# Sums of the seven half-size products' left operands: by VectorE, or by accumulating transfers

## The chip, the cores and the metric

One core of a Trainium2 chip runs the whole program. The metric is the device time of one execution in microseconds, from launch to end; less is better. The profile speaks of TensorE (PE, with PEld for its weight loads), VectorE (DVE), ScalarE (ACT), GpSimd (POOL) and SyncE (SP). SP does nothing here but issue transfers; POOL issues some too.

## The reference

One step of a decoder layer: a mixer (gated-delta heads and mLSTM heads), an output projection, and a feed-forward block with a short causal convolution. Only the last one matters here:

```python
h = _rmsnorm(x, norm_ffn_g)
u = jnp.einsum('bld,df->blf', h, w_up)          # 2048 -> 2 * 5632
uc, ffn_new = _causal_dwconv(u, ffn_buf, ffn_conv_w)
uc = uc + ffn_conv_b
gate, up = jnp.split(uc, 2, axis=-1)
x = x + jnp.einsum('blf,fd->bld', silu(gate) * up, w_down)   # 5632 -> 2048
```

There are 512 prompt tokens and 8 x 8 sample tokens, 576 columns in all, and everything is float32.

## The kernel before

Activations lie transposed: features on the 128 partitions, the 576 tokens (NT) as columns in two halves of 288 (HALF). A float32 product is made of three float32r products: each operand is split into a high part (a cast on ACT, line 120) and the rest (a subtraction on DVE, line 121), and high x high, high x low and low x high are summed in PSUM. A matmul takes a 128 x 128 weight block and 288 columns.

The feed-forward block has these stages. The first three pairs of up-projection tiles (gate tile j and up tile NF + j, NF = 44) are made directly (`dense`, the third pair by `dense_pair`, line 198). The other 41 pairs use Winograd's form of Strassen's scheme: the 2 x 2 blocks are the two output tiles by the two halves of the inner dimension (left operand A11, A12, A21, A22, each a 128 x 1024 array of w_up, 512 KB in DRAM) and the two inner halves by the two token halves (right operand). Seven products of half size take the place of eight. The down projection is cut into the BLOCKS of line 29: blocks of 4 tiles are made directly (`down`, line 198), two blocks of 12 by the same seven products (`down_seven`), in 8 groups each, with left blocks of 128 x 768 (384 KB).

The right operands (seven sums of activations, split, in the tiles bh and bl of pools b1 and b2) are made once per stage, by `prep` (up) and `down_prep` (down), mostly on DVE. The left operands are made group by group by the generator `left_operands`: each `yield` ends one step, which makes one of the group's seven operands: `op(src)` casts and splits it into wh and wl. Every third operand has wh and wl in the stage's own pool (`ur` or `sx`), the others in the two buffers each of pool `wp`. The operands that are sums are made by `comb` on DVE (line 1248): in order A11, S1 = A21 + A22, S2 = S1 - A11, A12, S3 = A11 - A21, S4 = A12 - S2, A22. The four blocks are loaded on SP's queue into tiles `raw`, two in `wp`, the rest in the stage's pool.

`product` (line 1287) multiplies the oldest waiting operand with right sum b (24 matmuls up, 18 down) and then runs the next step, so that operands are three ahead of the products. A buffer of wh and wl comes free when the product three back is done. `pair` runs the seven products of a pair in the order b = 0, 4, 5, 2, 1, 3, 6, adds their results up on DVE as they come (p1, u2, u3, u4 hold partial sums), puts them into the padded rows of `conv_pads` (filled by POOL), and runs the convolution (`conv_rest`) and `hidden`, whose result is stored to DRAM on SP's queue by `later`. `down_seven` does the same and adds into the residual tiles x2.

The stage is entered by `seven_start`: it closes the pool of the dense activations (`ap`), opens `b2` and `ur` in the memory that comes free, and runs the first three steps between parts of `prep`. The first three products of the first pair (operands 0, 1 and 2) are begun together, k blocks 0 to 4 of each and then 5 to 7 (KB1 = 5), because the right operands of the last k blocks are made last. In the down projection `down` runs the first three steps during its last three output pairs (mp >= 5).

PE's order is the program's (a manual schedule). On the other engines and queues a scheduler orders the instructions by priority and by when they could start; work under `urgent` or `ahead` has a higher priority.

Of the kernel before, what the change touches and what calls it, by code (L numbers as in the profile page):

```python
# [13 lines left out]
P = 128  # L14
# [54 lines left out]
class Layer:  # L69
# [1048 lines left out]
    def ffn(self):  # L1118
        nc, I, O = self.nc, self.I, self.O
        V, A, Pl = nc.vector, nc.scalar, nc.gpsimd  # L1120
        fin = I["ffn_conv"].rearrange("p (s j) b w -> p s j (b w)", s=2)
        fout = O["ffn_conv"].rearrange("p (s j) b w -> p s j (b w)", s=2)
        rv = None
        self.bh, self.bl = [], []
        for j in range(NPL):
            hs = []
            for s in range(2):
                if j < NPL - 1:
                    pd = self.dense()
# [24 lines left out]
        for j in range(NPL, NF):  # L1154
            if j == NF - 1:
                first = [self.load_hidden(self.ur.tile([P, NT], F32, tag="raw", name=self.nm("h"), bufs=4), i) for i in range(FB)]
# [60 lines left out]

    def operands(self):

        def raw(j, t, u):  # L1220
            pool, n = (self.wp, 2) if self.nraw % 6 < 2 else (self.ur, 4)
            self.nraw += 1
            r = pool.tile([P, 1024], F32, tag="raw", name=self.nm("raw"), bufs=n)
            self.nc.sync.dma_start(out=r, in_=self.I["w_up"][2 * j + t][u])
            return r

        return self.left_operands(self.ur, 1024, [lambda t, u, j=j: raw(j, t, u) for j in range(NPL, NF)])

    def left_operands(self, pool, width, raws):
        V = self.nc.vector  # L1230
        nop = 0

        def op(src):
            nonlocal nop
            with self.urgent():
                hl = []
                for n in "hl":
                    if nop % 3 == 2:
                        hl.append(pool.tile([P, width], F32R, tag="w" + n, name=self.nm("w" + n)))
                    else:  # L1240
                        hl.append(self.wp.tile([P, 1024], F32R, tag="w" + n, name=self.nm("w" + n), bufs=2)[:, 0:width])
                nop += 1
                self.split(*hl, src)
            self.ops.append(hl)

        def comb(out, a, b, o):
            with self.urgent():
                V.tensor_tensor(out=out, in0=a, in1=b, op=o)  # L1248

        nxt = [raws[0](*tu) for tu in ((0, 0), (1, 0))]  # L1250
        for i, raw in enumerate(raws):
            a11, a21 = nxt
            a22, a12 = raw(1, 1), raw(0, 1)
            op(a11)
            yield
            s = pool.tile([P, width], F32, tag="s", name=self.nm("s"))
            comb(s, a21, a22, ALU.add)
            op(s)
            yield
            comb(s, s, a11, ALU.subtract)  # L1260
# [12 lines left out]
            op(a22)  # L1273
            yield

    def part(self, out, b, op, k0, k1, nk):
# [15 lines left out]
    def pair(self, j, fst, steps):  # L1292

        V, A = self.nc.vector, self.nc.scalar
        add = lambda o, a, b: V.tensor_tensor(out=o, in0=a, in1=b, op=ALU.add)
        e = lambda tag: self.up.tile([P, HALF], F32, tag=tag, name=self.nm(tag))
        rg, og = self.conv_pads(fst[:, 0, j - NPL])
        ru, ou = self.conv_pads(fst[:, 1, j - NPL])

        def product(b):  # L1300
            if j == NPL and b in (0, 4, 5):
                return begun.pop(0)
            out = bank(b)
            self.product(out, b, steps)
# [3 lines left out]
            return self.psd()[:, 0, 0:HALF] if b in (4, 3) else self.psr()[:, 0:HALF]  # L1308

        if j == NPL:  # L1310
            begun = [bank(b) for b in (0, 4, 5)]
            for k0, k1 in ((0, KB1), (KB1, 8)):
                for out, b, op in zip(begun, (0, 4, 5), self.ops):
# [5 lines left out]
        def evac(outs, x, y):  # L1319
            with self.urgent():  # L1320
                for o, p, r in zip(outs, self.psum_parts(x, x), self.psum_parts(y, y)):
                    if o is not None:
                        add(o, p, r)
# [24 lines left out]
    def load_hidden(self, t, j):  # L1348
# [92 lines left out]
    def down_operands(self, ns):  # L1441
# [14 lines left out]
        return self.left_operands(self.sx, n, [lambda t, u, mp=mp: raw(mp, t, u) for mp in range(8)])  # L1456

    def down_seven(self, steps, ns, f1):
        V, A = self.nc.vector, self.nc.scalar
        add = lambda o, a, b: V.tensor_tensor(out=o, in0=a, in1=b, op=ALU.add)  # L1460
        e = lambda tag: self.sx.tile([P, HALF], F32, tag=tag, name=self.nm(tag))
        for mp in range(8):
            if mp == 5:
# [5 lines left out]
                self.product(out, b, steps, KS)  # L1469
                return out  # L1470

            def acc(o, *vs):
                for v in vs:
                    add(o, v, o)

            with self.urgent():
                p1, u2, u3, u4 = (e(t) for t in ("p1", "u2", "u3", "u4"))
                ps = product(0)
                A.copy(p1, ps)
                p5 = product(4)  # L1480
                ps = product(5)
                add(u2, ps, p1)
                add(u4, p5, u2)
                ps = product(2)
                acc(x[0][0], ps, p1)
                ps = product(1)
                add(u3, ps, u2)
                acc(x[1][1], ps, u4)
                ps = product(3)
                acc(x[0][1], ps, u4)  # L1490
                ps = product(6)
                acc(x[1][0], ps, u3)
        return hs

    def down_last(self, acts):
# [164 lines left out]
```

## Time and profile before

| | |
|---|---|
| time, median of 3 runs | 2697.01 us (2695.82 to 2698.49) |
| the profiled execution's own time | 2699.44 us |
| its span, first to last instruction | 2697.7 us |
| up projection by seven products | 1229.9 to about 2154 us of the span |
| down blocks by seven products | 2206.9 to 2342 and 2395.6 to 2528.7 us |
| plain loads of w_up | 176 of 512 KB |

Windows rows read: the stretch and its length, then busy time and instructions (x) of PE, PEld, DVE, ACT and POOL, then the granted clock, the share of the DMA engines and GB/s. A timeline row reads: start, duration, engine, line, operation, output <- inputs, shape, count, and in brackets how long the engine had been idle before it and what ended that. Matmuls overlap, so the distance between two starts is what one costs, not the duration shown. A row of a wait list reads: who <- for whom: us in total, times, longest.

### The profile page before, as it was taken

To read this page: it belongs to the slowest core of one execution; us is meant where nothing else is said; L and a number is where in the kernel's file an instruction comes from. 1 tells how busy PE (TensorE), PEld (TensorE's weight loads), DVE (VectorE), ACT (ScalarE), POOL (GpSimd) and SP (SyncE) were. 2 spreads that over 40 slices of the span, in tenths; PEclk is the share of its full clock that TensorE was granted. 3 is DMA by queue.
4 is the path that set the end of the run, shared out by engine and by line. 5 is a ranking of instruction groups with operands and counts; after the bars stand their busy time and mean duration, and the time that the engine had idled before them with its cause. 6 is when DMAs were issued, how large, how long until landed. Compare 5 with 4: busy or idle time off the path is not lost.

```text
span 2697.7 us, 48872 instructions
## 1 busy us (share of the span) xinstructions
PE 2651.0 (98%) x19967; PEld 2607.0 (97%) x19967; DVE 1994.0 (74%) x3338; ACT 1080.2 (40%) x1704; POOL 333.6 (12%) x658
## 2 busy tenths in 40 slices
PE   7999999999999999998999999999999999999998
PEld 7998999999999999998999999999999999999998
DVE  7887777765544332389888888888888888888646
ACT  5334344443333322254444444444444433433324
POOL 3222322222211001101000000000000100000001
PEclk9999999999999999999999999999999999999999
DMA  5222222222333344444333333333333373342333
GB/s 195 85 77 87 90 91 91 91 88 92 114 113 104 115 135 135 135 123 150 107 111 108 108 108 108 108 108 108 108 108 109 109 256 94 106 146 71 122 97 100
DMA packets 112233, 304.02 MB, mean 113 GB/s; under 512 B 21912, under 2 KB 28184, under 8 KB 112008
## 3 DMA queue, kind: packets, MB, share of 16 engines
q1 hardware_dynamic: 107896, 291.17, 34.0%
q0 software_dynamic: 1872, 7.37, 0.8%
q8 instruction: 156, 2.56, 0.4%
q10 hardware_dynamic: 2240, 2.36, 0.3%
q14 instruction: 69, 0.57, 0.1%
HBM read 264.79 MB, written 36.06 MB: 112 GB/s over the span
## 4 chain that ended last, share of the span: by engine, by line
PE 89%; DVE 4%; DMA 1%; issue 0%; ACT 0%; POOL 0%; DVEq 0%; POOLq 0%; SPq 0%; ACTq 0%
PE pd L198 36%; PE pr L1283 31%; PE pd L1283 12%; PE pr L198 3%; PE pr L1509 1%; DVE bl L121 1%; DVE wl L121 1%; DMA r<-hid 0%; DVE r L1544 0%; PE pr L256 0%; PE pr L843 0%; PE pr L980 0%; PE pr L982 0%; PE pr L690 0%; PE pr L687 0%
## 5 line engine op out<-in xcount | busy, mean ns | idle before, releaser
L120 ACT CAST wh<-raw 128x1024 fp32r<-128x1024 f32 (+1 forms) x394 | 404.6, 1027 | 741.1 <-PE pd L198 400.2
L1283 PE MATMUL pr<-bh,wh 128*128 128x288 f32 x2120 | 626.8, 296 | 1.9 <-ACT bh L120 1.9
L1283 PE MATMUL pr<-bh,wl 128*128 128x288 f32 x2120 | 624.6, 295 | 0.5 <-DVE wl L121 0.5
L1283 PE MATMUL pr<-bl,wh 128*128 128x288 f32 x2120 | 624.3, 294 | 0.6 <-DVE bl L121 0.6
L121 DVE TENSOR_TENSOR wl<-raw,wh 128x1024 fp32r<-128x1024 f32 (+1 forms) x394 | 476.5, 1210 | 178.8 <-ACT wh L120 172.4
L198 PE MATMUL pd<-ah,wh 128*128 128x288 f32 x2496 | 560.3, 306 | 0.0
L198 PE MATMUL pd<-ah,wl 128*128 128x288 f32 x2496 | 534.5, 296 | 0.2 <-DVE wl L121 0.2
L198 PE MATMUL pd<-al,wh 128*128 128x288 f32 x2496 | 533.8, 296 | 0.0
L198 PEld LDWEIGHTS pd<-ah,wh 128*128 128x128 f32 x2496 | 401.0, 189 | 14.2 <-issue 7.7
L198 PEld LDWEIGHTS pd<-ah,wl 128*128 128x128 f32 x2496 | 401.8, 189 | 0.5 <-DVE wl L121 0.5
L198 PEld LDWEIGHTS pd<-al,wh 128*128 128x128 f32 x2496 | 401.7, 189 | 0.0
L1283 PEld LDWEIGHTS pr<-bl,wh 128*128 128x128 f32 x2120 | 400.0, 189 | 1.1 <-DVE bl L121 1.1
L1283 PEld LDWEIGHTS pr<-bh,wh 128*128 128x128 f32 x2120 | 398.4, 188 | 2.1 <-ACT bh L120 2.1
L1283 PEld LDWEIGHTS pr<-bh,wl 128*128 128x128 f32 x2120 | 398.9, 188 | 1.2 <-DVE wl L121 1.2
L120 ACT CAST wh<-s 128x1024 fp32r<-128x1024 f32 (+1 forms) x171 | 169.6, 992 | 361.2 <-DVE s L1248 142.2
L1283 PE MATMUL pd<-bh,wh 128*128 128x288 f32 x848 | 252.2, 297 | 5.6 <-ACT wh L120 5.6
L1283 PE MATMUL pd<-bh,wl 128*128 128x288 f32 x848 | 250.8, 296 | 1.7 <-DVE wl L121 1.7
L1283 PE MATMUL pd<-bl,wh 128*128 128x288 f32 x848 | 249.7, 294 | 0.0
L121 DVE TENSOR_TENSOR wl<-s,wh 128x1024 fp32r<-128x1024 f32 (+1 forms) x171 | 196.5, 1149 | 26.0 <-ACT wh L120 18.4
L1283 PEld LDWEIGHTS pd<-bh,wh 128*128 128x128 f32 x848 | 160.3, 189 | 6.1 <-ACT wh L120 6.1
L1283 PEld LDWEIGHTS pd<-bh,wl 128*128 128x128 f32 x848 | 160.6, 189 | 2.2 <-DVE wl L121 2.2
L1283 PEld LDWEIGHTS pd<-bl,wh 128*128 128x128 f32 x848 | 161.0, 190 | 0.0
(400 smaller groups left out, 3501.1 us busy)
## 6 DMA issues: line engine op xcount, KB each, us to landing
raw<-in_w_up SPq DMA_DIRECT2D x176, 512.0 KB
raw<-in_w_in SPq DMA_DIRECT2D x114, 512.0 KB
raw<-in_w_down SPq DMA_DIRECT2D x40, 512.0 KB
raw<-in_w_out SPq DMA_DIRECT2D x32, 512.0 KB
raw<-in_w_down SPq DMA_DIRECT2D x40, 384.0 KB
hid<-r SPq DMA_DIRECT2D x44, 288.0 KB
r<-hid SPq DMA_DIRECT2D x40, 288.0 KB
r<-in_xT SPq DMA_DIRECT2D x32, 288.0 KB
```

What stands on the lines that cost most here:

```text
L120: nc.scalar.copy(hi, src)
L121: nc.vector.tensor_tensor(out=lo, in0=src, in1=hi.bitcast(F32), op=ALU.subtract)
L198: mm(outs[hf], w, x[:, hf * HALF:(hf + 1) * HALF], start=first and i == 0, stop=last and i == 2)
L1283: mm(out, w[:, ks], x[:, sl], start=k == 0 and i == 0, stop=k == nk - 1 and i == 2)
L1509: mm(pr[:, 0:n], w[:, ks], acts[kk][:, a * NT + sl.start:a * NT + sl.stop], start=kk == 0 and i == 0, stop=kk == FB - 1 and i == 2)
```

## The change

The four sums of a group are no longer made by DVE. A block is loaded into a tile, and another block is added to it by a second transfer that accumulates into the tile (`nc.gpsimd.dma_start(..., accum_op=ALU.add)`, on POOL's queue). Since such a transfer only adds, the operands are those of the same scheme with the first block row's sign turned: A11, S1 = A21 + A22, A12, S1 + A11, A11 + A21, A22, S1 + A11 + A12. The sums of the products subtract where they added, and the products run in the order b = 0, 4, 2, 5, 1, 6, 3. Tile `s` has two buffers, `raw` in `ur` three instead of four, and in `sx` one instead of two. A group has four plain loads, as before, and four accumulating ones besides, so that each group reads its blocks from DRAM twice.

```diff
     def operands(self):
 
-        def raw(j, t, u):
-            pool, n = (self.wp, 2) if self.nraw % 6 < 2 else (self.ur, 4)
+        def raw(i, t, u):
+            pool, n = (self.wp, 2) if self.nraw % 5 < 2 else (self.ur, 3)
             self.nraw += 1
-            r = pool.tile([P, 1024], F32, tag="raw", name=self.nm("raw"), bufs=n)
-            self.nc.sync.dma_start(out=r, in_=self.I["w_up"][2 * j + t][u])
-            return r
+            return pool.tile([P, 1024], F32, tag="raw", name=self.nm("raw"), bufs=n)
...
-        nxt = [raws[0](*tu) for tu in ((0, 0), (1, 0))]
-        for i, raw in enumerate(raws):
-            a11, a21 = nxt
-            a22, a12 = raw(1, 1), raw(0, 1)
+        def load(i, t, u, r=None):
+            r = raw(i, t, u) if r is None else r
+            nc.sync.dma_start(out=r, in_=src(i, t, u))
+            return r
+
+        def add(r, i, t, u):
+            nc.gpsimd.dma_start(out=r, in_=src(i, t, u), accum_op=ALU.add)
+
+        def sums(i):
+            return load(i, 1, 0, pool.tile([P, width], F32, tag="s", name=self.nm("s"), bufs=2))
+
+        s, a11 = sums(0), load(0, 0, 0)
+        add(s, 0, 1, 1)
+        for i in range(n):
+            a12 = load(i, 0, 1)
             op(a11)
             yield
-            s = pool.tile([P, width], F32, tag="s", name=self.nm("s"))
-            comb(s, a21, a22, ALU.add)
+            add(a11, i, 1, 0)
             op(s)
             yield
-            comb(s, s, a11, ALU.subtract)
+            add(s, i, 0, 0)
+            a22 = load(i, 1, 1)
+            op(a12)
+            yield
+            if i < n - 1:
+                nxt = sums(i + 1)
             op(s)
             yield
-            if i < len(raws) - 1:
-                nxt = [raws[i + 1](*tu) for tu in ((0, 0), (1, 0))]
-            op(a12)
+            add(s, i, 0, 1)
+            op(a11)
             yield
-            comb(a21, a11, a21, ALU.subtract)
-            op(a21)
+            if i < n - 1:
+                a11 = load(i + 1, 0, 0)
+                add(nxt, i + 1, 1, 1)
+            op(a22)
             yield
-            comb(s, a12, s, ALU.subtract)
             op(s)
-            yield
-            op(a22)
+            s = nxt
             yield
...
         p5 = product(4)
+        ps = product(2)
+        evac((og[0], None, None), ps, p1, ALU.add)
         ps = product(5)
         with self.urgent():
-            add(u2, ps, p1)
-            add(u4, p5, u2)
-        ps = product(2)
-        evac((og[0], None, None), ps, p1)
+            comb(u2, p1, ps, ALU.subtract)
+            comb(u4, p5, u2, ALU.subtract)
         ps = product(1)
-        evac((None, *ou[1:]), ps, u4)
         with self.urgent():
-            add(u3, ps, u2)
+            comb(u3, ps, u2, ALU.add)
+        evac((None, *ou[1:]), u4, ps, ALU.subtract)
+        ps = product(6)
+        evac((ou[0], None, None), ps, u3, ALU.subtract)
+        u = self.conv_rest(NF + j, ru, fst[:, 1, j - NPL])
         ps = product(3)
-        evac((None, *og[1:]), ps, u4)
+        evac((None, *og[1:]), ps, u4, ALU.subtract)
         g = self.conv_rest(j, rg, fst[:, 0, j - NPL])
-        ps = product(6)
-        evac((ou[0], None, None), ps, u3)
-        u = self.conv_rest(NF + j, ru, fst[:, 1, j - NPL])
         self.hidden(j, g, u, rg)
...
         def raw(mp, t, u):
             if mp % 2 and mp < 7:
-                r = self.act.tile([P, 2 * NT], F32R, tag="f", name=self.nm("f"), bufs=FB).bitcast(F32)[:, 0:n]
-            elif u == 0:
-                r = self.wp.tile([P, 1024], F32, tag="raw", name=self.nm("raw"), bufs=2)[:, 0:n]
-            else:
-                r = self.sx.tile([P, n], F32, tag="raw", name=self.nm("raw"), bufs=2)
-            self.nc.sync.dma_start(out=r, in_=src[mp, t, u])
-            return r
+                return self.act.tile([P, 2 * NT], F32R, tag="f", name=self.nm("f"), bufs=FB).bitcast(F32)[:, 0:n]
+            if t == u:
+                return self.wp.tile([P, 1024], F32, tag="raw", name=self.nm("raw"), bufs=2)[:, 0:n]
+            return self.sx.tile([P, n], F32, tag="raw", name=self.nm("raw"))
```

In `pair` the three products begun together are now those of b = 0, 4 and 2. `down_seven` gets the same order of products and the same signs, with the sums taken into x2. The four hidden tiles that are loaded at the last pair of the up projection go to three buffers of `raw` and one of `s`.

More of the change, by code (lines that the diff above doesn't have):

```diff
@@ L1155, in ffn @@
             if j == NF - 1:
-                first = [self.load_hidden(self.ur.tile([P, NT], F32, tag="raw", name=self.nm("h"), bufs=4), i) for i in range(FB)]
+                first = [self.load_hidden(self.ur.tile([P, NT], F32, tag=t, name=self.nm("h"), bufs=n), i)
+                         for i, (t, n) in enumerate((("raw", 3), ("raw", 3), ("raw", 3), ("s", 2)))]
             self.pair(j, fst, steps)
@@ L1236, in op @@
                 hl = []
-                for n in "hl":
+                for c in "hl":
                     if nop % 3 == 2:
-                        hl.append(pool.tile([P, width], F32R, tag="w" + n, name=self.nm("w" + n)))
+                        hl.append(pool.tile([P, width], F32R, tag="w" + c, name=self.nm("w" + c)))
                     else:
-                        hl.append(self.wp.tile([P, 1024], F32R, tag="w" + n, name=self.nm("w" + n), bufs=2)[:, 0:width])
+                        hl.append(self.wp.tile([P, 1024], F32R, tag="w" + c, name=self.nm("w" + c), bufs=2)[:, 0:width])
@@ L1242, in op @@
                 nop += 1
-                self.split(*hl, src)
+                self.split(*hl, t)
             self.ops.append(hl)
-        def comb(out, a, b, o):
-            with self.urgent():
-                V.tensor_tensor(out=out, in0=a, in1=b, op=o)
-        nxt = [raws[0](*tu) for tu in ((0, 0), (1, 0))]
-        for i, raw in enumerate(raws):
-            a11, a21 = nxt
-            a22, a12 = raw(1, 1), raw(0, 1)
+        def load(i, t, u, r=None):
+            r = raw(i, t, u) if r is None else r
+            nc.sync.dma_start(out=r, in_=src(i, t, u))
+            return r
@@ L1294, in pair @@
         V, A = self.nc.vector, self.nc.scalar
-        add = lambda o, a, b: V.tensor_tensor(out=o, in0=a, in1=b, op=ALU.add)
+        comb = lambda o, a, b, op: V.tensor_tensor(out=o, in0=a, in1=b, op=op)
         e = lambda tag: self.up.tile([P, HALF], F32, tag=tag, name=self.nm(tag))
@@ L1300, in product @@
         def product(b):
-            if j == NPL and b in (0, 4, 5):
+            if j == NPL and b in (0, 4, 2):
                 return begun.pop(0)
@@ L1310, in pair @@
         if j == NPL:
-            begun = [bank(b) for b in (0, 4, 5)]
+            begun = [bank(b) for b in (0, 4, 2)]
             for k0, k1 in ((0, KB1), (KB1, 8)):
-                for out, b, op in zip(begun, (0, 4, 5), self.ops):
+                for out, b, op in zip(begun, (0, 4, 2), self.ops):
                     self.part(out, b, op, k0, k1, 8)
@@ L1322, in evac @@
                     if o is not None:
-                        add(o, p, r)
+                        comb(o, p, r, op)
         p1, u2, u3, u4 = (e(t) for t in ("p1", "u2", "u3", "u4"))
@@ L1480, in down_seven @@
                 p5 = product(4)
+                ps = product(2)
+                for v in (ps, p1):
+                    comb(x[0][0], v, x[0][0], ALU.add)
                 ps = product(5)
[L1482 to L1485, printed above, removed]
+                comb(u2, p1, ps)
+                comb(u4, p5, u2)
                 ps = product(1)
-                add(u3, ps, u2)
-                acc(x[1][1], ps, u4)
+                comb(u3, ps, u2, ALU.add)
+                comb(x[1][1], x[1][1], ps)
+                comb(x[1][1], x[1][1], u4, ALU.add)
+                ps = product(6)
+                comb(x[1][0], ps, x[1][0], ALU.add)
+                comb(x[1][0], x[1][0], u3)
                 ps = product(3)
-                acc(x[0][1], ps, u4)
-                ps = product(6)
-                acc(x[1][0], ps, u3)
+                comb(x[0][1], ps, x[0][1], ALU.add)
+                comb(x[0][1], x[0][1], u4)
         return hs
```

17 lines of the change are left out of this document (7 added, 10 removed).

## The prediction

> **What bounds the kernel now.** I read the page's first part, then the windows by stage, then the PE timeline where a window leaves PE below 100%, then the queues that feed those places.
>
> ```profile
> PE 2651.0 (98%) x19967; PEld 2607.0 (97%) x19967; DVE 1994.0 (74%) x3338; ACT 1080.2 (40%) x1704; POOL 333.6 (12%) x658
> ...
> 1240.00:1300.00 60.00, 57.06 (x416) 56.12 (x416) 57.40 (x82) 28.61 (x36) 6.71 (x19) 0.98 0.40 128
> 1300.00:1400.00 100.00, 100.00 (x757) 100.00 (x756) 88.30 (x118) 42.97 (x50) 5.43 (x28) 1.00 0.34 103
> 1400.00:1500.00 100.00, 100.00 (x757) 100.00 (x756) 89.58 (x117) 43.90 (x51) 5.49 (x26) 1.00 0.38 115
> ...
> 2200.00:2300.00 100.00, 97.64 (x726) 96.93 (x725) 89.00 (x138) 37.52 (x52) 1.07 (x2) 0.98 0.39 120
> ```
>
> TensorE is the bound: 98% of the span. In the steady part of the seven-product stage it is busy 100 of 100 us, with 757 matmuls, one every 0.132 us. VectorE, at 88%, is nearly full there but waits for TensorE, not the other way. The change leaves the number of matmuls alone. So in this stage it can win nothing; it can only lose, if an operand comes late. What can be won lies where the stage starts, and the timeline of PE has two such places:
>
> ```profile
> 1229.93 0.29 PE L1283 MATMUL pr<-bh,wh 128*128 128x288 f32 x1
> ...
> 1231.78 0.29 PE L1283 MATMUL pr<-bh,wl 128*128 128x288 f32 x1
> 1236.09 0.61 PE L1283 MATMUL pd<-bh,wh 128*128 128x288 f32 x1 [4.01 <-ACT wh L120]
> ...
> 1238.51 0.44 PE L1283 MATMUL pd<-bl,wh 128*128 128x288 f32 x1
> 1238.75 0.44 PE L1283 MATMUL pd<-bh,wl 128*128 128x288 f32 x1
> ...
> 1244.60 0.29 PE L1283 MATMUL pr<-bh,wl 128*128 128x288 f32 x1
> 1246.75 0.40 PE L1283 MATMUL pr<-bh,wh 128*128 128x288 f32 x1 [1.85 <-ACT bh L120]
> ...
> 1251.43 0.40 PE L1283 MATMUL pr<-bh,wl 128*128 128x288 f32 x1 [0.48 <-DVE wl L121]
> ...
> 2206.87 0.29 PE L1283 MATMUL pr<-bh,wh 128*128 128x288 f32 x1
> ...
> 2211.31 0.40 PE L1283 MATMUL pd<-bh,wh 128*128 128x288 f32 x1 [1.60 <-ACT wh L120]
> ...
> 2212.57 0.61 PE L1283 MATMUL pd<-bh,wl 128*128 128x288 f32 x1 [0.73 <-DVE wl L121]
> ...
> 2216.05 0.29 PE L1283 MATMUL pr<-bh,wh 128*128 128x288 f32 x1
> ```
>
> Start 1 (the up projection) begins at 1229.93 with the first passes (k 0 to 4) of three products begun together; 15 matmuls in, PE waits 4.01 us for the second operand, S1. After the wait matmuls come 0.24 us apart (1238.51 to 1238.75) for some 6 us. The 75th matmul starts at 1251.43 instead of 1229.93 + 74 x 0.132 = 1239.7: 11.7 us lost. Start 2 (first down block): 36 matmuls from 2206.87 should end at 2211.6, and the next product begins at 2216.05: 4.4 us lost. So 16 us, 0.6%, is all that this change could win. Start 3 (second down block, 2395.55) loses nothing today.
>
> **The change, part by part.**
>
> ```profile
> L121 DVE TENSOR_TENSOR wl<-s,wh 128x1024 fp32r<-128x1024 f32 x81 | 99.3, 1226 | 16.2 <-ACT wh L120 12.7
> L1248 DVE TENSOR_TENSOR s<-raw,raw 128x1024 f32<-128x1024 f32 x27 | 33.1, 1225 | 0.9
> ...
> L1248 DVE TENSOR_TENSOR s<-s,f 128x768 f32<-128x768 f32 x3 | 2.9, 952 | 0.0
> ...
> fst<-in_ffn_conv POOLq DMA_DIRECT2D x1, 738.0 KB, 5.5
> ...
> fst<-in_ffn_conv POOLq DMA_DIRECT2D x1, 54.0 KB, 2.4
> ...
> 2104.61 0.20 POOL L1098 COPY fst<-r 128x18 f32<-128x18 f32 x1 [8.68 <-DVE r L1295]
> ...
> 2179.36 0.54 POOL L1408 DMA_DIRECT2D r<-x2d  x1 [16.27 <-ACT bh L120]
> ```
>
> Removed: four DVE sums a group, 41 x 4 x 1.22 + 16 x 4 x 0.95 = 261 us of VectorE. In the steady part their price is nothing, as PE hides them. The signs cost nothing: pair still has 9 evacuations and down_seven 11, add or subtract. The new product order holds p5's bank one product longer, with two pd banks and the other pd product now last. The gate's conv_rest now comes last, so hidden and its store come about 0.7 us later; what is queued behind that store on SP are loads whose buffers come free two products (6 us) or more before their cast.
>
> Added: four accumulating DMAs a group on POOL's queue, 4 x (41 + 16) = 228 in all, at 0.54 us of POOL each: 2.2 us in a group's 22.3. Behind them on POOL wait the pads and state copies, which have idle time to give (8.7 us before the copy at 2104.61). Plain loads stay four a group.
>
> What decides is the time L from issue to landing of an accumulate; no row shows one. From below: a plain 512 KB load on SP landed in 3.5 us (below). Loads on POOL took 2.4 us for 54 KB and 5.5 us for 738 KB, 4.5 ns per KB. An accumulate must also read what it adds to: counted as two passes, 2.4 + (1024 - 54) x 0.0045 = 6.8 us; as three, 9.1. I take 5.5, the 738 KB row, which lies between one pass and two; for 384 KB 2.4 + 0.75 x 3.1 = 4.7, with 3.2, 5.6 and 7.4 as the other cases. The Trainium skill (Collectives: The Full Stack, "The bandwidth ceiling: the fold count and why AG ≠ RS ≠ AR") says that a reducing transfer runs at half a copy's rate because it needs two source reads; that is the 6.8, no run here shows it yet, and by it the sum below would be +5.3.
>
> Steady part. The tightest sum is S1 + A11: its accumulate can go once S1's low part is made, and must land before the cast two operands on.
>
> ```profile
> 1505.84 1.05 ACT L120 CAST wh<-s 128x1024 fp32r<-128x1024 f32 x1 [2.16 <-PE pd L1283]
> ...
> 1506.92 1.23 DVE L121 TENSOR_TENSOR wl<-s,wh 128x1024 fp32r<-128x1024 f32 x1 [0.47 <-ACT wh L120]
> ...
> L120 ACT CAST wh<-s 128x768 fp32r<-128x768 f32 x20 | 16.7, 836 | 35.0 <-DVE s L1248 16.7 <-PE pd L1283 10.7 <-PE pr L1283 7.6
> ...
> 2094.37 9.55 PE pr L1283 x72
> ...
> 2417.27 7.11 PE pr L1283 x54
> ```
>
> A cast starts when the buffer three operands back comes free, two products (3.18 us each) before its own product. S1's cast at 1505.84 means S1's product at 1512.1, its low part done at 1508.1, and the product of the next sum at 1518.5. Less 2.2 us of split, plus 0.26 until the low part is read, the sum must be there by 1516.4: 8.3 us for POOL and L. With 0.1 + 5.5 (6.8) it holds. In the down blocks a product is 2.37 us and the split 0.84 + 0.95: 4 x 2.37 - 3.4 = 6.1 us, against 4.7 (5.6). It holds, barely in the second case. The other accumulates have 9 us or more. So the steady price is 0.
>
> Start 1.
>
> ```profile
> 1213.57 0.33 SPq L1224 DMA_DIRECT2D raw<-in_w_up  x1
> ...
> 1219.92 10.54 SPq L1224 DMA_DIRECT2D raw<-in_w_up  x2
> ...
> SPq L1224 <- PE pd L198: 9.8, 1, 9.8
> ...
> 1233.65 1.23 DVE L1248 TENSOR_TENSOR s<-raw,raw 128x1024 f32<-128x1024 f32 x1
> ```
>
> Today A11 and A21 come early (1213.57, 1219.92) into wp; A22's load, the first tile of pool ur, waits 9.8 us until the last dense matmul lets go of that memory, goes at 1230.1 and has landed by 1233.65. In the changed code S1 starts from A21 in tag s, now the first tile of ur, so I take it that its load waits likewise. Then the accumulate of A22 follows it, where one DVE sum of 1.13 us stood: 1233.65 + 0.1 + 5.5 + 1.05 for the cast = 1240.3, 4.2 us later than 1236.09. From there the first passes take 8.65 us as today (1236.09 to 1244.74, one step after the row of 1244.60; the slow matmuls are in it): 1248.9; the second passes no longer wait, since three sums fewer (3.4 us) stand ahead of their bh and bl; the 75th matmul starts 29 x 0.132 later, at 1252.8: **+1.3 us**. (L 3.5: -0.6; 6.8: +2.6; 9.1: +4.9.)
>
> Start 2.
>
> ```profile
> 2206.59 0.43 PE L198 MATMUL pd<-f,wl 128*128 128x288 f32 x2
> ...
> 2210.43 0.83 ACT L120 CAST wh<-s 128x768 fp32r<-128x768 f32 x1
> ```
>
> S1's parts need a buffer that the last dense product frees at 2207.0 (2206.59 + 0.43). Today its cast comes at 2210.43 behind DVE work; now S1 can have landed long before, so 2207.0 + 0.1 + 0.84 + 0.95 = 2208.9, before its product at 2209.25: the 4.4 us go. Late next is S1 + A11: 2208.9 + 0.1 + 4.7 + 1.8 = 2215.5, due 2206.87 + 54 x 0.132 + 0.26 = 2214.3: 1.2, with slow matmuls after it, about 2.0. **-2.4 us** (-4.4; -0.8; +1.1).
>
> Start 3.
>
> ```profile
> 2395.55 2.42 PE pr L1283 x18
> 2397.97 2.38 PE pd L1283 x18
> ```
>
> The same chain from 2395.55: 2397.4 + 4.8 + 1.8 = 2404.0 against 2402.9: 1.1, with slow matmuls **+1.9 us** (0; +3.5; +5.4).
>
> Sum +0.8 us on the profiled execution's 2699.44; that execution is 2.4 above the median of the three runs, so 2697.01 + 0.8 = **2697.8**. Bounds: all L short, -5; two passes, +5.3.
>
> **The rivals.**
>
> A, the late sum (slower). If L passes 8.3 us up, or 6.1 us down, every group waits: one us over costs 40 + 14 = 54 us. At three passes 0.8 x 40 + 1.3 x 14 = 50, and the starts +11: 2758; lesser excesses lie between. For it: never measured here; two accumulates and a plain load can be under way at once; POOL is in order, and an accumulate behind a copy that waits for an evacuation comes later. Against: the windows. 0.18.
>
> B, the DMA engines become the bound. The four transfers add 94 GB/s at the source; with two passes the share of 0.34 at 103 GB/s would scale to 0.34 x 291 / 103 = 0.96, with three to 1.27: 28.3 us a group, +6 x 41, some 2940. Against it stand these rows, where slices of nine tenths carry some 400 GB/s:
>
> ```profile
> DMA  0805845758000000788999531000850058998810
> GB/s 25 227 6 113 326 191 113 250 176 296 28 0 13 0 0 0 145 285 184 420 406 384 111 131 43 0 0 0 176 227 0 0 91 324 400 368 262 280 79 0
> ```
>
> 0.05.
>
> C, faster by over 0.2%. If S1's tile lies where memory is free early, its two transfers end before 1230, the 4.0 us wait and the slow matmuls after it go, and with fewer sums ahead of bh and bl start 1 gains up to 8; with start 2's 4.4 that is 2685. Against: the 9.8 us wait of the first ur tile. 0.10.
>
> D, POOL held up by VectorE. The row of 2179.36 took 0.54 us with DVE nearly full, so I count none. If each issue waited out a DVE instruction (1.2 or 0.95 us), 5.6 + 0.95 passes 6.1 by 0.4: 14 x 0.4 and some 4 us at the starts, 2707. The Trainium skill (SBUF — State Buffer, "Summary: rules for kernel authors") warns that descriptors written by GpSimd starve while VectorE is in its fast modes; no run here shows it. 0.05.
>
> That the gain is not there at all is my forecast itself: the relieved engine was not the bound.
>
> **How the numbers follow.** Forecast 0.62, A 0.18, C 0.10, B 0.05, D 0.05. 0.2% (5.4 us) is about what a measurement of this kernel can tell from no change. Of the forecast, 0.05 falls below -5.4 and 0.10 above +5.4 (two passes with queueing), 0.47 within. Faster 0.05 + 0.10 = 0.15; same 0.47; slower 0.10 + 0.18 + 0.05 + 0.05 = 0.38. Forecast alone: 2691 to 2704. The range 2688 to 2735 takes in half of A and of C, and D; left out are 0.09 + 0.05 + 0.05 = 0.19.
>
> **What would show it.** Right: 757 matmuls per 100 us in the stage, DVE near 66% there; accumulates landing in 5 to 7 us; S1's first cast at 1239 to 1241; no 4.4 us at start 2. Wrong: PE waiting for "ACT wh" once a group (A), DMA share near 1 (B), POOL issues over 1 us (D), S1 cast before 1230 (C).

## The result, and the profile after

The changed kernel takes 2942.98 us (median of 4 runs, 2940.69 to 2947.57) against 2696.60 us for the kernel before (4 runs, 2695.82 to 2698.49): 1.0912 times as long, 95% interval 1.0899 to 1.0926. That lies far outside the forecast range of 2688 to 2735. Some 240 us have come from somewhere.

The page of the changed kernel, its first line, the costliest groups of the stage, and two rows of its list of transfers (size, median us from issue to landing):

```profile
PE 2746.7 (93%) x19967; PEld 2675.8 (91%) x19967; DVE 1737.6 (59%) x3110; ACT 1076.9 (37%) x1704; POOL 601.5 (20%) x886
...
L1294 PE MATMUL pr<-bh,wh 128*128 128x288 f32 x2120 | 662.5, 313 | 112.7 <-ACT wh L120 112.6
L1294 PE MATMUL pr<-bh,wl 128*128 128x288 f32 x2120 | 660.1, 311 | 27.9 <-DVE wl L121 26.5
...
s<-in_w_up POOLq DMA_DIRECT2D x123, 512.0 KB, 6.6
...
raw<-in_w_up POOLq DMA_DIRECT2D x41, 512.0 KB, 5.5
```

VectorE has lost 1994.0 - 1737.6 = 256 us of work (261 were forecast), and TensorE has the same 19967 matmuls, yet it now waits 112.6 us for the high part of an operand ("ACT wh") and 26.5 for a low part. The windows of the up projection, 800 us of it, first before and then after:

```profile
1300.00:2100.00 800.00, 800.00 (x6038) 800.00 (x6037) 711.52 (x935) 348.14 (x396) 43.67 (x216) 1.00 0.35 108
```

```profile
1300.00:2100.00 800.00, 733.30 (x5183) 719.12 (x5182) 461.95 (x680) 300.05 (x341) 197.20 (x306) 0.95 0.71 174
```

TensorE falls from 6038 to 5183 matmuls in the same time and stands idle for 67 us; the granted clock falls to 0.95. The DMA engines are busy for 0.71, so they are not the bound, and VectorE is down to 58%. No engine is full: it is a chain of waits. The stages, from the start of the first matmul to the end of the last in the timeline of PE, in us:

| | up | down, 1st block | down, 2nd block | span |
|---|---|---|---|---|
| before | 924.9 | 137.5 | 133.3 | 2697.7 |
| after | 1074.0 | 185.0 | 176.6 | 2938.9 |

The three stages lose 149.1 + 47.5 + 43.3 = 239.9 of the span's 241.2. When the distances between the starts of neighbouring matmuls in these stages are added up against 0.132 us, gaps over 0.3 us have grown by 176 us (189 after, 13 before) and spacings between 0.15 and 0.3 us by 66 (69 after, 3 before): **waits, and matmuls at half rate behind the waits**. Sorted by the product that they precede, 105 of the 119 us of waits in the up projection, and 35 of 37 and 32 of 33 in the down blocks, stand at the product of S1 + A11. One sum of the four is late, in nearly every group.

One group shows how. The timeline of the changed kernel around S1 of a group, all engines:

```profile
1523.57 0.33 SPq L1249 DMA_DIRECT2D s<-in_w_up  x1
...
1525.06 1.05 ACT L120 CAST wh<-s 128x1024 fp32r<-128x1024 f32 x1 [1.82 <-PE pr L1294]
...
1525.77 0.86 POOL L1253 DMA_DIRECT2D raw<-in_w_up  x1 [0.24 <-DVE wl L121]
...
1526.14 1.23 DVE L121 TENSOR_TENSOR wl<-s,wh 128x1024 fp32r<-128x1024 f32 x1 [0.30 <-ACT wh L120]
...
1527.46 1.75 POOL L1253 DMA_DIRECT2D s<-in_w_up  x2 [0.83 <-DMA s<-in_w_up]
...
1538.56 1.04 ACT L120 CAST wh<-s 128x1024 fp32r<-128x1024 f32 x1 [8.22 <-DMA s<-in_w_up]
1539.64 1.22 DVE L121 TENSOR_TENSOR wl<-s,wh 128x1024 fp32r<-128x1024 f32 x1 [7.46 <-ACT wh L120]
1539.66 0.40 PE L1294 MATMUL pr<-bh,wh 128*128 128x288 f32 x1 [1.84 <-ACT wh L120]
1540.92 0.40 PE L1294 MATMUL pr<-bh,wl 128*128 128x288 f32 x1 [0.73 <-DVE wl L121]
...
1550.36 1.06 ACT L120 CAST wh<-s 128x1024 fp32r<-128x1024 f32 x1 [0.89 <-PE pr L1294]
```

S1 is cast at 1525.06 and its low part is done at 1527.37. POOL starts three accumulates within 2.3 us: A11 + A21 of this group (raw), then the row with x2, which in the order that the scheduler gave POOL is first the **next** group's S1 + A22 and only then this group's S1 + A11. (The source writes these two the other way round; E6 below shows POOL waiting for a load with S1's low part done.) That row waited for a landing: A21 of the next group, which SP could issue only at 1523.57, as its tile `s` came free then. The next group's S1 is not cast before 1550.36, so its accumulate had 23 us. S1 + A11 is the third of three in POOL's queue, and its sum is cast at 1538.56, 13.5 us after S1's cast. The prediction's window was 10.56 us from cast to cast (1505.84 to 1516.4): it is missed by 2.9. PE's two waits in these rows, from the starts, are 2.13 - 0.13 = 2.0 (1537.53 to 1539.66) and 1.02 - 0.13 = 0.9 (1539.89 to 1540.92): again 2.9.

Of the four accumulates of a group, in POOL's order, the time from issue to landing has these medians in the up projection: A11 + A21 5.5 us, next S1 + A22 6.4, S1 + A11 9.5 (7.8 to 10.8 in all but two groups), S1 + A12 6.3.

### The profile page after: what moved, and what is told of

It is laid out like the page before. It is cut to its first block, busy times and chain, and to the rows that moved or that the text cites. A ratio compares the mean times of both kernels' runs of the same rounds, so it can differ in the third digit from the quotient of the medians.

```text
span 2938.9 us, 49185 instructions
## 1 busy us (share of the span) xinstructions
PE 2746.7 (93%) x19967; PEld 2675.8 (91%) x19967; DVE 1737.6 (59%) x3110; ACT 1076.9 (37%) x1704; POOL 601.5 (20%) x886
## 5 line engine op out<-in xcount | busy, mean ns | idle before, releaser
L1294 PE MATMUL pr<-bh,wh 128*128 128x288 f32 x2120 | 662.5, 313 | 112.7 <-ACT wh L120 112.6
L1294 PE MATMUL pr<-bh,wl 128*128 128x288 f32 x2120 | 660.1, 311 | 27.9 <-DVE wl L121 26.5
L1294 PE MATMUL pr<-bl,wh 128*128 128x288 f32 x2120 | 653.8, 308 | 0.0
L1294 PEld LDWEIGHTS pr<-bh,wh 128*128 128x128 f32 x2120 | 428.1, 202 | 124.0 <-ACT wh L120 123.9
L1294 PEld LDWEIGHTS pr<-bh,wl 128*128 128x128 f32 x2120 | 427.7, 202 | 42.8 <-DVE wl L121 42.8
L1294 PEld LDWEIGHTS pr<-bl,wh 128*128 128x128 f32 x2120 | 429.1, 202 | 0.0
L1253 POOL DMA_DIRECT2D s<-in_w_up x123 | 107.0, 941 | 415.7 <-DVE wl L121 361.0
L1098 POOL COPY fst<-r 128x18 f32<-128x18 f32 x88 | 93.2, 1059 | 434.9 <-DVE r L1306 371.2
```

The lines of the kernel that those rows point to most:

```text
L1098: nc.gpsimd.tensor_copy(f, rb[:, 512:602].rearrange("p (b w) -> p b w", b=9)[:, :, 0:2])
L1253: nc.gpsimd.dma_start(out=r, in_=src(i, t, u), accum_op=ALU.add)
L1294: mm(out, w[:, ks], x[:, sl], start=k == 0 and i == 0, stop=k == nk - 1 and i == 2)
```

## Experiments

The theory: the accumulate itself is as quick as forecast, but S1 + A11 stands behind others on POOL. Rivals: an accumulate is too slow wherever it stands; the DMA engines cannot carry the doubled reads; or the other order of products and the signs cost something. The stages of all kernels (us, as above), and their times:

| | up | down 1 | down 2 | time, median | against before |
|---|---|---|---|---|---|
| before | 924.9 | 137.5 | 133.3 | 2696.60 | |
| after | 1074.0 | 185.0 | 176.6 | 2942.98 | 1.0912 (1.0899 to 1.0926) |
| E1, urgent first | 930.3 | 158.2 | 149.6 | 2743.04 (2 runs) | 1.0175 (1.0136 to 1.0214) |
| E2, plain | 924.8 | 145.9 | 137.9 | 2712.19 (1 run) | |
| E3, only tight | 923.2 | 158.3 | 155.2 | 2742.24 (1 run) | |
| E6, no A11 + A21 | 1046.0 | 177.3 | 170.7 | 2895.39 (1 run) | |
| E8, next behind | 934.0 | 167.1 | 159.5 | 2763.60 (1 run) | |
| E9, splits ahead | 932.3 | 158.9 | 150.9 | 2742.65 (1 run) | |
| E10, low first | 921.8 | 151.5 | 146.0 | 2724.45 (1 run) | |
| E4, split | 928.2 | 144.9 | 136.9 | 2712.76 (3 runs) | 1.0061 (1.0038 to 1.0084) |
| E5, up only | 931.0 | 136.8 | 133.3 | 2704.59 (7 runs) | 1.0030 (1.0019 to 1.0041) |
| E7, early first | 931.6 | 134.0 | 133.3 | 2700.01 (11 runs) | 1.0012 (1.0003 to 1.0020) |

Beside them the kernel before took 2695.76 us (E1 to E4), 2697.02 (E5, E6, E7, E9) and 2698.44 (E8, E10). The two executions of E1 lie 8.6 us apart and the seven of E5 8.1, so single runs are read by their stages. E2, E3, E6 and E10 leave sums out, as their edits show.

### E1: the order on POOL alone

```diff
-            add(a11, i, 1, 0)
             op(s)
             yield
-            add(s, i, 0, 0)
+            first = add(s, i, 0, 0)
+            add(a11, i, 1, 0, first)
...
-            add(s, i, 0, 1)
+            second = add(s, i, 0, 1)
...
-                add(nxt, i + 1, 1, 1)
+                add(nxt, i + 1, 1, 1, second)
```

The fourth argument makes POOL issue the accumulate behind the one named, by `tc.issue_after`.

> Same transfers and bytes as the changed kernel; only POOL's order differs: S1 + A11 goes first, A11 + A21 behind it, the next group's S1 + A22 behind S1 + A12. Theory Q (the tight accumulate queues behind two others that have time to spare): S1 + A11 lands 5.5 to 7 us after its issue instead of 10 to 11, inside the window of 8.3 us; a group of the up projection goes from 26.2 back to 22.3 to 23 us; time 2697 to 2740. Rival R1 (one accumulate alone is too slow for the window): over 2850, groups of 25 us or more. Rival R2 (the 16 DMA engines have not the capacity for twice the bytes): over 2850, since the bytes are the same.

The window of E1 over the same 800 us:

```profile
1300.00:2100.00 800.00, 799.89 (x6036) 799.51 (x6035) 547.57 (x792) 352.31 (x395) 240.50 (x360) 1.00 0.82 203
```

With the same transfers and bytes, TensorE is full again (6036 matmuls, granted clock 1.00), at a higher share of the DMA engines (0.82) than in the changed kernel. S1 + A11 lands in a median of 5.5 us. The up projection gets back 144 of its 149 us, the down blocks 27 of 47 and 27 of 43; the whole is 3 us above the range expected. That the engines cannot carry it is refuted for the up projection; so is an accumulate that is too slow by itself.

### E2: the same transfers, not accumulating

```diff
-            nc.gpsimd.dma_start(out=r, in_=src(i, t, u), accum_op=ALU.add)
+            nc.gpsimd.dma_start(out=r, in_=src(i, t, u))
```

> The changed kernel with plain overwriting transfers in place of the accumulating ones, in the same order on POOL; the sums are left out, so that the operands are single blocks. Q: a transfer occupies the engines for half as long; three in a row land in 2.4 + 3 x 1.5 = 7 us, inside 8.3: up groups of 22.3 us, down groups near 16.6 (5.9 us against 6.1); time 2697 to 2725. If it is the issue on POOL or the landing by itself and not the second pass that costs: as the changed kernel, over 2900. R2: recovers as well.

In the changed kernel's own order the up projection is back at 924.8 us, with TensorE full over the 800 us:

```profile
1300.00:2100.00 800.00, 800.00 (x6039) 800.00 (x6038) 558.91 (x790) 355.86 (x395) 193.28 (x360) 1.00 0.64 203
```

So the new order of products, the signs and the added issues on POOL cost nothing there; what costs is accumulating in that order on POOL. In the down blocks 8.4 and 4.6 us are left even so. The list of transfers of E2, and the queue's line (packets, MB, share of the engines over the span) of E2 and then of E1:

```profile
q0 software_dynamic: 30608, 118.54, 14.2%
...
s<-in_w_up POOLq DMA_DIRECT2D x123, 512.0 KB, 4.4
raw<-in_w_up POOLq DMA_DIRECT2D x41, 512.0 KB, 3.8
```

```profile
q0 software_dynamic: 34704, 118.54, 24.0%
```

Before the change this queue had 7.37 MB and 0.8% (22 us of the engines' time). The 111 MB more take 0.142 x 2710.4 - 22 = 363 us as plain transfers and 0.240 x 2737.0 - 22 = 635 us as accumulating ones, 1.75 times as much. The Trainium skill's rule (Collectives: The Full Stack, "The bandwidth ceiling: the fold count and why AG ≠ RS ≠ AR"), half a copy's rate for a collective's reducing transfer, comes near to this for the engines' time; for the landing of one transfer the same pair of rows gives 5.5 against 3.8, 1.4 times.

### E3: only the two tight accumulates

```diff
-        add(s, 0, 1, 1)
...
-            add(a11, i, 1, 0)
...
-                add(nxt, i + 1, 1, 1)
```

> Only the two accumulates into S1 (A11, A12) stay; the additions of A22 to S1 and of A21 to A11 are left out. Q: nothing stands ahead of S1 + A11, it lands in 5 to 6.5 us; up groups 22.3 us; time 2695 to 2715. R1: groups stay over 24 us, time over 2800. R2: recovers too (half of the added bytes), so this run does not tell R2 from Q.

Up 923.2 us: with nothing ahead of it S1 + A11 lands in 5.4 us and no group waits. The whole, 2742.24 us, is a miss (2695 to 2715 expected): the down blocks keep 158.3 and 155.2 with nothing queued ahead, and S1 + A11 landing in 4.8. PE waits there for S1 + A11 (9 and 11 us in all) and for S1 + A11 + A12 (8 and 7). In the down blocks something else is late as well; E10 takes that up.

### E6 and E8: which of the two ahead of it

E6 leaves out A11 + A21, the first of the three:

```diff
-            add(a11, i, 1, 0)
```

> The changed kernel in its own order on POOL, with A11 + A21 left out, so that one accumulate instead of two stands ahead of S1 + A11. Queue theory: S1 + A11 lands in 6.5 to 8 us instead of 9.6, the up stage falls from 1074 to 925 to 960 us; the down blocks stay late (140 to 170 us each); time 2720 to 2790. If the place in the queue does not matter: the up stage stays over 1040 us.

A miss: the up projection was expected back near 925 to 960 us and takes 1046.0, in the range set down for "the place in the queue does not matter". The timeline of E6 around S1 shows why that does not follow:

```profile
1513.52 0.33 SPq L1249 DMA_DIRECT2D s<-in_w_up  x1
...
1515.95 1.23 DVE L121 TENSOR_TENSOR wl<-s,wh 128x1024 fp32r<-128x1024 f32 x1 [0.16 <-ACT wh L120]
...
1517.82 1.75 POOL L1253 DMA_DIRECT2D s<-in_w_up  x2 [2.33 <-DMA s<-in_w_up]
...
1527.20 1.05 ACT L120 CAST wh<-s 128x1024 fp32r<-128x1024 f32 x1 [7.05 <-DMA s<-in_w_up]
```

S1's low part is done at 1517.18, and POOL has waited since 1515.5 for A21 of the next group to land (issued at 1513.52), because that group's S1 + A22 still stands ahead. Then the two go together, and the second lands 9.3 us later. So the run took away the accumulate that matters less. E8 therefore alters only the place of the next group's S1 + A22, and leaves A11 + A21 first:

```diff
-            add(s, i, 0, 1)
+            second = add(s, i, 0, 1)
...
-                add(nxt, i + 1, 1, 1)
+                add(nxt, i + 1, 1, 1, second)
```

> The changed kernel with one thing altered: POOL issues the next group's S1 + A22 behind this group's S1 + A12, not ahead of S1 + A11; A11 + A21 stays first, and all sums are made. Theory (the hoisted accumulate of the next group, with its wait for the load of A21, is what holds S1 + A11 up): S1 + A11 lands in 5.5 to 8 us, within the window of 8.3, and the up projection goes from 1074 back to 925 to 945 us, the whole to some 2735 to 2760. Rival (any accumulate ahead of S1 + A11 is enough, A11 + A21 too): it stays above 1000 us in the up projection, the whole above 2820.

```profile
1530.44 0.86 POOL L1254 DMA_DIRECT2D raw<-in_w_up  x1 [0.24 <-DVE wl L121]
1531.03 1.05 ACT L120 CAST wh<-s 128x1024 fp32r<-128x1024 f32 x1 [2.15 <-PE pr L1295]
...
1533.63 0.86 POOL L1254 DMA_DIRECT2D s<-in_w_up  x1 [2.33 <-DVE wl L121]
...
1539.13 1.05 ACT L120 CAST wh<-s 128x1024 fp32r<-128x1024 f32 x1 [2.82 <-DMA s<-in_w_up]
```

S1 + A11 now goes 0.3 us after S1's low part, and its cast follows S1's by 8.1 us in place of 13.5. The up projection takes 934.0 us, in the range expected (the whole is 4 us above its own). In it S1 + A11 has 8.7 us from cast to cast as a median, against 8.2 in E1, so A11 + A21 ahead of it costs about half a microsecond and is borne. The accumulate of the **next** group, put ahead by the scheduler, is the cause of 140 of the 149 us: it has 23 us in the rows of the changed kernel and goes first all the same, and it waits for a load. Its place costs more than that wait: from E1 to the changed kernel the landing of S1 + A11 grows from 5.5 to 9.5 us, and its issue after S1's low part only from 0.3 to 1.0 (medians).

### E9 and E10: the rest of the down blocks

E9 is E1 with the splits at a higher priority, `self.ahead(4 * PRIO)` in place of `self.urgent()` in `op`.

> All sums by transfers, S1 + A11 first on POOL, and the splits of left operands ahead of the evacuations on DVE and ACT. If the down blocks lose because S1's low part stands 2.6 us behind evacuations on DVE (so that 3.5 us are left of 6.1 for a transfer of 4.8): the blocks fall from 158 and 150 us to 140 to 150 and 135 to 145, time 2712 to 2730. If the transfer alone is too long there, they stay, 2735 or more.

A miss, 2742.65 us and 158.9 and 150.9 in the down blocks: the low part of S1 started a median of 1.5 us after its cast in the down blocks, no sooner than in E1 (1.3). The priority did not move what stood ahead, so the run tells nothing about the cause. The timeline of VectorE in E3 shows what stands ahead (S1's cast is at 2490.55 there). The rows of line 1465 are evacuations, which take a product out of PSUM into its sums:

```profile
2490.82 0.45 DVE L1465 TENSOR_TENSOR u<-pd,u 128x288 f32<-128x288 f32 x1
2491.19 0.45 DVE L1465 TENSOR_TENSOR u<-pr,u 128x288 f32<-128x288 f32 x1
2491.55 0.45 DVE L1465 TENSOR_TENSOR r<-r,pr 128x288 f32<-128x288 f32 x1
2491.91 0.95 DVE L121 TENSOR_TENSOR wl<-raw,wh 128x768 fp32r<-128x768 f32 x1
2492.78 0.45 DVE L1465 TENSOR_TENSOR r<-r,u 128x288 f32<-128x288 f32 x1
2493.15 0.45 DVE L1465 TENSOR_TENSOR r<-pr,r 128x288 f32<-128x288 f32 x1
2493.64 0.46 DVE L1465 TENSOR_TENSOR r<-r,u 128x288 f32<-128x288 f32 x1
2494.01 0.95 DVE L121 TENSOR_TENSOR wl<-s,wh 128x768 fp32r<-128x768 f32 x1
```

E10 is E3 with the two evacuations of product 6 (2493.15 and 2493.64) forced behind this low part:

```diff
                 ps = product(6)
-                comb(x[1][0], ps, x[1][0], ALU.add)
-                comb(x[1][0], x[1][0], u3)
+                with self.tc.issue_after(self.low.ins):
+                    comb(x[1][0], ps, x[1][0], ALU.add)
+                    comb(x[1][0], x[1][0], u3)
```

> The kernel with only S1 + A11 and S1 + A12 by accumulates (A21 + A22 and A11 + A21 left out), and in the down blocks the two evacuations of product 6 are put behind the low part of the next group's S1 on VectorE, two instructions of 0.37 to 0.45 us per group. Before, this low part started a median of 3.0 us after its cast in place of 0.87. Theory (the down blocks lose because the low part queues behind evacuations): each group gains 0.75 us or a little more, so the down blocks go from 158.3 and 155.2 to some 148 to 152 and 145 to 150, the whole to some 2725 to 2733. Rival (the landing alone is too long and the queue on VectorE only follows from the waits): 156 to 160 and 153 to 157, the whole 2738 to 2744.

The low part starts 2.2 us after its cast (median) in place of 3.1, and the down blocks go from 158.3 and 155.2 to 151.5 and 146.0, as this theory expected; the whole is a little below its range. Of the 16 us gained, 8 are waits at S1 + A11 and 8 at S1 + A11 + A12, the next sum of the same tile. So in the down blocks the window itself is short, since the low part of S1 queues behind VectorE's evacuations. Four evacuations and one other low part still stand ahead; they were not moved. In E1 that queue is shorter (1.3 us), and yet the blocks take 158.2 and 149.6 us, with 14 and 13 us of waits at S1 + A11 and A11 + A21; how this divides between the window and the other accumulates under way was not told apart.

### E4: the tight sums on VectorE, the others by accumulates

```diff
-            add(s, i, 0, 0)
+            comb(s, s, a11)
+            add(a11, i, 1, 0)
...
-            add(s, i, 0, 1)
+            comb(s, s, a12)
```

> S1 + A11 and + A12 by VectorE as before the change, A21 + A22 and A11 + A21 by accumulating transfers; all sums are made. The two transfers have 13 us or more. Q and R1: no wait per group, 22.3 us; start 2 gains 2 to 4 us, start 1 loses 1 to 5; time 2693 to 2703. R2: two accumulates a group fit the engines' time; same.

2712.76 us, above the 2693 to 2703 expected; up 928.2, and the down blocks lose only 7.4 and 3.6 us. The remaining waits of PE at the first down block:

```profile
2210.96 0.40 PE L1298 MATMUL pd<-bh,wh 128*128 128x288 f32 x1 [1.35 <-ACT wh L120]
2212.26 0.40 PE L1298 MATMUL pd<-bh,wl 128*128 128x288 f32 x1 [0.76 <-DVE wl L121]
...
2220.64 0.40 PE L1298 MATMUL pr<-bh,wh 128*128 128x288 f32 x1 [1.26 <-ACT wh L120]
2221.64 0.40 PE L1298 MATMUL pr<-bh,wl 128*128 128x288 f32 x1 [0.46 <-DVE wl L121]
```

The first pair is S1, which start 2 was to be rid of; the second is A11 + A21, the accumulate now next in tightness. About half of VectorE's relief is given back (636 of 800 us busy in the up projection, against 548 in E1 and 712 before), and the kernel is still 0.6% behind the one before.

### E5 and E7: no down blocks, and an early first sum

E5 has E1's order up and the down blocks as before the change. E7 is E5 with the first group's S1 = A21 in an early tile of `wp`, and its wh and wl in `ur`:

```diff
-                    if nop % 3 == 2:
+                    if nop % 3 == 1:
...
-        s, a11 = sums(0), load(0, 0, 0)
+        a11 = load(0, 0, 0)
+        s = load(0, 1, 0)
```

> Transfers in the up projection alone, with S1 + A11 first on POOL; the down blocks as before the change (sums, order of products and signs). If the rest of the loss with S1 + A11 first (46 us) is what its trace shows, 5 us at start 1 and 37 us in the down blocks: the up stage takes 928 to 931 us, the down blocks 137 and 133 again, time 2699 to 2704. If something else of the transfers costs time outside these places: over 2710.

> The kernel of the run with transfers in the up projection alone, and the first group's S1 in an early tile of wp, its split in the buffers of ur, so that S1 needs not wait for the last dense matmul. If that wait set start 1: the first wait of 4 us (11 in the changed kernel) falls under 1.5 us, PE then waits for the last right operands instead, the up stage takes 919 to 924 us (925 before), time 2690 to 2696. If the right operands alone set start 1: 925 us, 2697.

E5 keeps one loss, where the up projection begins: 931.0 against 924.9 us, of which 2.3 us at start 1 (by the 75th matmul) and 3.0 in waits for two sums of the second group. Its median time, 2704.59, is just above the range expected (2699 to 2704); the profiled execution is the shortest of the seven, 2699.14. E7 takes the wait for S1 at start 1 away, and PE's waits there become these:

```profile
1229.78 0.40 PE L1343 MATMUL pd<-bh,wh 128*128 128x288 f32 x1 [0.21 <-ACT wh L120]
...
1247.03 0.61 PE L1343 MATMUL pr<-bh,wh 128*128 128x288 f32 x1 [7.65 <-ACT bh L120]
```

The wait for S1 has gone to 0.2 us, but PE then waits 7.65 us for the right operands of the last k blocks (bh). A window of E7 and a row of VectorE show what those wait for; the second window is the kernel before:

```profile
1235.50:1243.60 8.10, 3.08 (x19) 2.39 (x18) 4.33 (x10) 1.68 (x3) 0.00 (x0) 0.84 1.03 301
...
1243.60 0.82 DVE L1198 SCALAR_TENSOR_TENSOR y<-y,par,rstd 128x576 f32<-128x576 f32 x1 [3.77 <-DMA y<-x2d]
```

```profile
1238.20:1243.30 5.10, 5.10 (x24) 4.84 (x24) 5.10 (x9) 3.31 (x5) 1.12 (x3) 0.57 0.32 94
```

VectorE stands idle for 3.77 us until the activations y land, from a load issued at 1235.57. Before the change that load was issued at 1238.20 and VectorE took it up at 1243.32 without a wait. While it is under way the DMA engines are full in E7 (1.03; a share is counted by when packets start, so it can pass 1), and at 0.32 before. So the second wait comes at least in part from the transfers of this stage's start, which the change made heavier; no run took them away to show it. The stage takes 931.6 us, outside both ranges expected (919 to 924, and 925), 2.7 us of it in waits for two sums of the second group, as in E5. E7 is the fastest of the kernels with accumulates in the up projection, at 2700.01 us (ratio 1.0003 to 1.0020); none beats the kernel before.

## Why the prediction was wrong

**What bounds the kernel: held.** TensorE at full rate in the stage, VectorE at 88% waiting for it. E2 and E3 have TensorE at 800.00 of 800 us with VectorE at 70%: the 261 us removed are worth nothing in the steady part, as forecast (256 were measured).

**The time of one accumulate: held.** L was set at 5.5 and 4.7 us. With nothing ahead of it S1 + A11 lands in 5.4 and 4.8 (E3), first in the queue in 5.5 and 4.8 (E1). The value was chosen between one pass and two, not derived, so that it fits so well is in part luck.

**"Steady part": this is the step that failed.** "The other accumulates have 9 us or more. So the steady price is 0." The window of 8.3 us was right (the 2.9 us by which the rows above miss it are what PE waits), and it was set against L of one accumulate. But POOL's queue was never put in order: accumulates that have time to spare can stand ahead of the one that has none. The prediction asked what stands behind an accumulate on POOL, and not what the tightest stands behind. Third in the queue, S1 + A11 took 9.5 us (8.1 in the down blocks), and PE waited in nearly every group. With the matmuls at half rate that follow, this is nearly all of the loss.

**The window of the down blocks** (6.1 us) was mis-sized besides. It let the low part follow its cast at once (0.84 us); in the changed kernel it starts 2.4 us after it (median of the two blocks), in E3 3.1, behind evacuations. Its handing to POOL takes 0.3 us in place of 0.1. That leaves 3.6 to 4.3 us for L = 4.8.

**The clock was left out for waits within groups.** Half-rate matmuls after waits were counted at the starts alone. They make 66 of the 241 us.

**Start 1** (forecast +1.3). The 75th matmul starts 25.25 us after the first in the changed kernel, 21.50 before: +3.8. The rows of the changed kernel:

```profile
1232.71 0.90 POOL L1253 DMA_DIRECT2D s<-in_w_up  x1 [0.81 <-DMA s<-in_w_up]
...
1241.40 1.04 ACT L120 CAST wh<-s 128x1024 fp32r<-128x1024 f32 x1 [7.20 <-DMA s<-in_w_up]
...
1242.49 0.61 PE L1294 MATMUL pd<-bh,wh 128*128 128x288 f32 x1 [11.88 <-ACT wh L120]
```

The load of A21 waited for the memory and had landed by 1232.7, as forecast; the accumulate behind it took 8.6 us, not 5.5. While it was under way the DMA engines were full (1.03):

```profile
1232.70:1241.30 8.60, 0.00 (x0) 0.00 (x0) 3.98 (x8) 0.43 (x1) 1.76 (x2) 0.65 1.03 287
```

That the other transfers of the starting stage made the difference is therefore likely, but no run took them away.

**Start 2** (forecast -2.4). The premise failed: "S1 can have landed long before". Landed or not, its cast stands behind a cast of right operands on ACT, as before:

```profile
2357.80 0.43 ACT L120 CAST bh<-r 128x288 fp32r<-128x288 f32 x1 [3.55 <-DVE r L1207]
...
2358.14 0.83 ACT L120 CAST wh<-s 128x768 fp32r<-128x768 f32 x1
...
2359.02 0.40 PE L1294 MATMUL pd<-bh,wh 128*128 128x288 f32 x1 [1.59 <-ACT wh L120]
```

The stage starts at 2354.85, so the cast comes 3.3 us later, against 3.6 before the change (2206.87 to 2210.43). Of the 4.4 us that were to go, 1.5 went: the 37th matmul is 2.96 us late, against 4.43.

**Start 3** (forecast +1.9). Nothing is lost up to the 37th matmul, as forecast, but the first wait for S1 + A11 has the steady size: the prediction had the mechanism and, again, L of one. (By the chain of start 2 its first sum would come at 2397.6, not 2397.4; the 0.2 us decide nothing.)

**The rivals.** A had the mechanism (PE waits for "ACT wh" once a group), and named an accumulate that comes later on POOL; its price rule, 40 + 14 groups for each us over, gives 104 us up and 59 down with the mean waits for S1 + A11, 2.6 and 4.2 us a group. With the 66 us at half rate that makes 229 of the 241. But it was priced by the number of passes, up to 2758, and not by places in a queue. B's figure, some 2940, was hit by another road: its own sign, a DMA share near 1, stands at 0.71 over the 800 us, and E1 moves the same bytes with PE full; only at start 1 are the engines full. C and D did not come: S1's first cast is after 1230 (E7 brings it ahead, and nothing is gained), and a single accumulate held POOL for 0.86 us, more than the 0.54 counted but under D's 1 us.

## What to carry to other kernels

When work moves to a queue that runs in order, write that queue's order down before pricing it, and price the tightest item by its place, with what those ahead of it wait for; slack in the others is no help if they go first. A scheduler may put the next round's work ahead of this round's, so tie the urgent transfer's place by hand. And a chain's window is as long as its in-order engines let it be: check what stands before each of its small steps.

## What the hardware showed that was not expected

A wait of some 2.6 us can cost 1.5 us more. The windows of the changed kernel just after one (PE waits 1.92 and 0.72 us before 1514.13):

```profile
1515.00:1518.50 3.50, 3.50 (x17) 3.50 (x16) 2.44 (x3) 0.60 (x1) 0.23 (x1) 0.52 0.83 183
1518.50:1522.00 3.50, 3.50 (x28) 3.50 (x28) 0.91 (x2) 0.77 (x1) 0.00 (x0) 0.99 1.00 336
```

In the first window the granted clock is 0.52: for 3.36 us (1515.16 to 1518.52) matmuls come 0.24 us apart, 14 of them, 1.5 us lost. After the like wait at 1539.66 and 1540.92 no such stretch follows. The Trainium skill (TensorE: Matmul & The Clock Gate, "Part 1: The HAM clock gate (the "warmup" mystery)") tells of a gate that halves the clock after an idle window of about 3.4 us, counted in windows that run freely. The length and the rate agree with it. An idle window there is not: PE stood idle for 2.64 us, in two pieces with two matmuls between them, and the measurement decides. Free-running windows would explain why only some waits are followed by it, which no run here shows.

An accumulating transfer of 512 KB into SBUF lands in 5.4 us by itself, against 3.8 to 4.4 for a plain one on the same queue, and takes 1.75 times the engines' time. Two issued together land one after the other: 5.5 us for the first in the queue, and some 9 for one that follows at once (A11 + A21 in E1: 9.1).
